# Hybrid SSD and attention block: decay sums placed behind z, one group's norm factors a weight run later, rotary channels swapped by two transfers

## The chip, the cores and the metric

The kernel runs on one core of one Trainium2 chip. The metric is the device time of one execution in microseconds (us), as the median of three runs. The profile is of one further execution.

## The reference

One layer over 256 tokens of width 1024, in float32. An RMS norm is followed by one wide input projection whose columns feed two branches and their gates: a Mamba-2 mixer (8 groups, 32 heads, two chunks of 128 tokens) and an attention with partial rotary embedding (16 heads of 64 channels). Both branches are projected, weighted with sigmoid gates, added, projected once more and added to the input; a gated conv FFN of width 2816 and a last norm follow. Cut to what the change touches:

```python
dt = softplus(dt_raw + dt_bias);  A = -exp(a_log)
A_cs = cumsum(dt * A)                      # inside each chunk of 128 tokens
L = exp(A_cs[l] - A_cs[s])  for s <= l     # decay factors of the scan
y = ssd_scan(X, dt, A, B, C) + X * d_skip
y = y * silu(z)
y = y * rsqrt(mean(y * y over the group's 256 channels) + eps) * norm_w

rot, rest = t[..., :16], t[..., 16:]       # q and k, per head of 64 channels
rot_half = concat([-rot[8:], rot[:8]])
t = concat([rot * cos + rot_half * sin, rest])
```

The attention uses q and k only in the product over a head's 64 channels, so any order of these channels serves if it is the same in q and k.

## The kernel before

Channels lie on the 128 partitions and tokens along the free axis. Weights stream from HBM in units of 1 MB (`raw`, eight tiles of 128 x 256 columns, three buffers, loaded by SP in the order of `seq`). Each unit is split in two halves: ScalarE copies the rounded part (`hi`, line 94) and VectorE subtracts it (`lo`, line 95); there are four buffers of each, that is two units. The split of a unit is traced two units ahead (`next_unit`). A product takes three matmuls for each tile, hi times hi, hi times lo and lo times hi (lines 151 to 153 with the weight as the stationary operand, 169 to 171 with the tokens stationary). So a unit of `mm_unit` is 48 matmuls with 256 columns.

TensorE's order is the order of the program (`manual_schedule`). On VectorE, ScalarE and GpSimd a planner chooses the order when the kernel is built; a block under `high_priority` goes ahead of other work that is ready, and `issue_after` puts instructions behind a named one. Each of these engines then works off its own list in that order.

For each of eight groups g TensorE runs `u_bc` (B and C), `u_x`, the small matmuls `small_1`, `u_qk`, then `u_z`, and in odd groups `u_v`, in even groups a quarter of the gates in four steps (`u_gate`: two units, each step one half unit), with `small_2` between them. `small_1(g)` works on the scan output of the group before (`s_y`), its scores (`a_s`), and, one group further back, on the attention output (`a_o`) and the norm factors (`s_pb`). `small_2(g)` has the score products and decay factors of the scan (`s_cb`), the transposed x (`s_xt`), the sums of squares of the group before (`s_st`) and its transposed probabilities (`a_t`).

Group 0 is special, since the decay sums are made there for all heads. `dt_chain` (line 483) computes `dtw` on VectorE from u_x(0) on, `dt_sums` (line 508) sums it over tokens with the matmuls of lines 510 and 511, `dt_turn` (line 516) transposes the sums, copies them to `acsT` (line 521) and sends them to HBM (line 522); `load_acs` (line 302) reads the rows of a group back to all partitions (`acsB`, one buffer, line 304). `s_cb` makes twelve decay steps per group from `acsB` on ScalarE (lines 365 and 367) and one over all (368). TensorE's order in group 0 is u_bc(0), the dt matmuls, u_x(0), u_qk(0), `dt_sums`, u_z(0), `dt_turn`, steps 1, 2, 3 of the gate, `small_2(0)`, step 4. The bias of the gates is loaded on GpSimd's queue right behind the swap transfers (line 585, two of 1 MB).

The norm factors of a group come in two steps. `s_st` sums squares and starts a chain of small VectorE steps that ends in `ry` (line 195). `s_pb` spreads `ry` over the partitions with two fp32 matmuls into `pb` (line 215, four instructions in the trace); VectorE multiplies (line 408) and the result is split into `yn` (lines 177 and 178). Behind the last group come `small_1(8)`, the first run of `w_ssd` (which uses `yn` 0 to 3), `small_2(8)`, the second run, `s_pb(7)`, `a_o(7)`, and the third and fourth; `yn` of group 6 is used in the fourth.

The rotation is done in `u_qk` and `turn_qk`. ScalarE copies q and k to `qkraw` (line 311), GpSimd issues DMAs that write the partner rows into `swap` (lines 314 and 315), and VectorE multiplies by cosine (318), and later by sine (325), and adds (326). Before, the 16 rotated channels of a head are its first 16 rows, partners 8 rows apart.

Of the kernel before, what the change touches and what calls it, by code (L numbers as in the profile page):

```python
# [18 lines left out]
P = 128  # L19
# [3 lines left out]
NG = 8  # L23
# [16 lines left out]
def block_kernel(tc, xtok_d, par_d, nf_d, con_d, rope_d, wdt_d, win_d, wgate_d, bg_d, watt_d, wssd_d, wout_d, wup_d, wdn_d, out_d):  # L40
    nc = tc.nc
    st = ExitStack()
    pool = lambda name, bufs=1, **kw: st.enter_context(tc.tile_pool(name=name, bufs=bufs, **kw))
    with st:
        const = pool("const")
        wpool = pool("w")
        pairs = pool("pairs")
# [8 lines left out]
        rope = const.tile([P, 2, T], F32, name="rope")  # L56
# [249 lines left out]
        def u_qk(g):  # L306
            hv = next_unit()
            ps = mm_tile()
            mm_unit(ps, hv, hn)
            raw = atp.tile([P, 2, T], F32, tag="qkraw", bufs=1, name="qkraw")  # L310
            S[g]["qk_copy"] = nc.scalar.activation(raw, ps, AF.Copy)
            sw = swaps[g % 2]
            for o in (0, 64):
                nc.gpsimd.dma_start(sw[o : o + 8], raw[o + 8 : o + 16])
                nc.gpsimd.dma_start(sw[o + 8 : o + 16], raw[o : o + 8])
            qk = S[g]["qk"] = atp.tile([P, 2, T], F32, tag="qk", bufs=2, name="qk")
            cosb = rope[:, 0:1, :].to_broadcast([P, 2, T])
            nc.vector.tensor_tensor(qk, raw, cosb, op=ALU.mult)

        def turn_qk(g):  # L320

            sw, qk = swaps[g % 2], S[g]["qk"]
            sinb = rope[:, 1:2, :].to_broadcast([P, 2, T])
            with tc.issue_after(split_unit.last.ins):
                nc.vector.tensor_tensor(sw, sw, sinb, op=ALU.mult)
                nc.vector.tensor_tensor(qk, qk, sw, op=ALU.add)
# [77 lines left out]
        def s_pb(g):  # L404
            rb = rms_bcast(S[g]["ry"])
            yg = S[g]["yg"]
            for m in range(2):
                nc.vector.scalar_tensor_tensor(yg[:, m], yg[:, m], col(C_NW + 2 * g + m), rb, op0=ALU.mult, op1=ALU.mult)
                p = new_pair("yn")
                split_pair(p, yg[:, m])  # L410
                yn[2 * g + m] = p
# [27 lines left out]
        def a_t(g):  # L439
            S[g]["pt"] = []  # L440
            for j in range(2):
                pt_ps = ps_s.tile([P, 4, P], F32, tag="at", bufs=2, name="pt_ps")
                for b in range(3):
                    nc.tensor.transpose(pt_ps[:, b], S[g]["pr"][j][:, b], ident)  # L444
                pt = atp.tile([P, 3, P], F32, tag="pt", bufs=2, name="pt")
                nc.scalar.activation(pt, pt_ps[:, 0:3], AF.Copy)
                S[g]["pt"].append(pt)
# [60 lines left out]
        def dt_sums():  # L508
            ps_a = ps_s.tile([P, 2, T], F32, tag="ss", bufs=2, name="ps_a")
            nc.tensor.matmul(ps_a[:, 0, 0 : 2 * NH], tri, dtw[:, 3], start=True, stop=True)  # L510
            nc.tensor.matmul(ps_a[:, 0, 2 * NH : 3 * NH], ones, dtw[:, 3, 0:NH], start=True, stop=True)
            with tc.high_priority():
                nc.vector.tensor_copy(flat(acs), ps_a[:, 0, 0 : 2 * NH])
                nc.vector.tensor_tensor(alm, ps_a[:, 0, 2 * NH : 3 * NH], acs[:, 0, :], op=ALU.subtract)
# [45 lines left out]
        def small_1(g):  # L560
            if 0 <= g - 1 < NG:
                s_y(g - 1)
                a_s(g - 1)
            if 0 <= g - 2:
                a_o(g - 2)
                s_pb(g - 2)

        def small_2(g):
            if g < NG:
                s_cb(g)  # L570
                s_xt(g)
            if 0 <= g - 1:
                s_st(g - 1)
                a_t(g - 1)

        for g in range(NG):
            if g:
                u_bc(g)
                u_x(g)
                small_1(g)  # L580
                load_acs(g)
            u_qk(g)
            if g == 0:
                for c in range(2):
                    tc.keep_in_program_order(nc.gpsimd.dma_start(gates[:, c], bg_d.partition_broadcast(P)))
                dt_sums()
                u_z(g)
                turn_qk(g)
                dt_turn()
                load_acs(0)  # L590
                gate = u_gate(0)
                next(gate)
                next(gate)
                next(gate)
                small_2(g)
                next(gate)
            elif g == NG - 1:
                u_z(g)
                turn_qk(g)
                small_2(g)  # L600
                u_v(g)
            elif g % 2:
                u_v(g)
                turn_qk(g)
                u_z(g)
                small_2(g)
            else:
                u_z(g)
                turn_qk(g)
                gate = u_gate(g // 2)  # L610
                next(gate)
                next(gate)
                small_2(g)
                next(gate)
                next(gate)
# [216 lines left out]
def _layout(i):  # L832

    f = {k: np.asarray(v) for k, v in i.items()}
    rows = lambda a: np.ascontiguousarray(a)
    vec = lambda a: a.reshape(-1, P).T
    cw = f["ssd_conv_w"][0]
    fw = f["ffn_conv_w"][0]
    par = np.concatenate(
        [  # L840
            vec(f["norm1_w"][0]), vec(f["norm2_w"][0]), np.zeros((P, 8), np.float32),
            vec(f["ssd_norm_w"][0]), vec(np.repeat(f["ssd_d"][0], 64)),
            cw.reshape(4, 32, P).transpose(2, 1, 0).reshape(P, 128), vec(f["ssd_conv_b"][0]),
            fw.reshape(3, NF, P).transpose(2, 1, 0).reshape(P, 3 * NF), vec(f["ffn_conv_b"][0]),
            np.broadcast_to(f["ssd_dt_bias"][0], (P, NH)), np.broadcast_to(f["ssd_a_log"][0], (P, NH)),
        ],
        axis=1,
    )
    w = f["w_in"][0]
    oz, ox, odt = 0, 2048, 6144  # L850
    oq = odt + NH
    ok, ov, og = oq + 1024, oq + 2048, oq + 3072
    a = np.arange(P)
    b = np.arange(256)
    units = np.zeros((5, NG, 256), np.int64)
    for g in range(NG):
        units[0, g] = np.r_[ox + 2048 + g * P + a, ox + 3072 + g * P + a]
        units[1, g] = ox + 256 * g + b
        units[2, g] = np.r_[oq + g * P + a, ok + g * P + a]
        units[3, g] = ov + 256 * (g % 4) + b  # L860
        units[4, g] = oz + 256 * g + b
    cols = units.reshape(-1, 256)

    def tiles(wm, cols):

        n = cols.shape[0]
        return rows(wm[:, cols.reshape(-1)].reshape(-1, P, n, 256).transpose(2, 1, 0, 3))

    def tiles512(wm):

        n = wm.shape[1] // 512
        return rows(wm.reshape(-1, P, n, 512).transpose(2, 1, 0, 3)).reshape(n, P, -1, 256)

    up = np.stack([np.r_[m * P + a, FH + m * P + a] for m in range(NF)])
    s, l = np.arange(P)[:, None], np.arange(P)[None, :]
    tri = (s <= l).astype(np.float32)
    neg = np.where(l <= s, np.float32(0), np.float32(-1e30)).astype(np.float32)
    con = np.stack([np.eye(P, dtype=np.float32), tri, np.ones((P, P), np.float32), tri, neg, np.zeros((P, P), np.float32), neg], axis=1)
    con = np.concatenate([con.reshape(P, 7 * P), np.tile(np.eye(NH, dtype=np.float32), (4, 1))], axis=1)
    inv = np.float32(500000.0) ** (-np.arange(0, 16, 2, dtype=np.float32) / np.float32(16))  # L880
    ang = np.arange(T, dtype=np.float32)[:, None] * inv[None, :]
    rope = np.zeros((P, 2, T), np.float32)
    rope[:, 0] = 1.0
    for o in (0, 64):
        rope[o : o + 8, 0] = rope[o + 8 : o + 16, 0] = np.cos(ang).T
        rope[o : o + 8, 1] = -np.sin(ang).T
        rope[o + 8 : o + 16, 1] = np.sin(ang).T
    return [
        ("xtok", f["x"][0].reshape(2, P, D).transpose(1, 0, 2)),
        ("par", par),  # L890
        ("nf", f["norm_f_w"]),
        ("con", con),
        ("rope", rope),
        ("wdt", w[:, odt : odt + NH].reshape(KD, P, NH).transpose(1, 0, 2)),
        ("win", tiles(w, cols).reshape(5, NG, P, KD, 256)),
        ("wgate", tiles512(w[:, og : og + 2 * D])),
        ("bg", f["b_gate"][0]),
        ("watt", tiles512(f["w_att_proj"][0])),
        ("wssd", tiles512(f["w_ssd_proj"][0])),
        ("wout", tiles512(f["w_out"][0])),  # L900
        ("wup", tiles(f["w_ffn_up"][0], up)),
        ("wdn", tiles512(f["w_ffn_down"][0])),
    ]
# [18 lines left out]
```

## Time and profile before

| | |
|---|---|
| median of 3 runs | 609.34 us (609.33 to 609.73) |
| the profiled execution | 610.12 us, of which the span is 608.3 |
| busy: TensorE / weight load | 592.5 us (97%) / 547.1 us (90%) |
| busy: VectorE / ScalarE / GpSimd | 463.2 us (76%) / 361.7 us (59%) / 26.5 us (4%) |
| mean granted TensorE clock | 0.99 |
| DMA | 109.79 MB, 180 GB/s over the span |

The span is the time from the first to the last instruction. Busy shares are means over stages with different limits, so the waits of the busiest engine, and what ended them, are read next, then the timelines of the engines around those waits. A timeline row gives the start, the duration, the engine, the line, what is written and read, and in brackets how long the engine had been idle and what ended it. TensorE's matmuls are pipelined, so the time between two starts tells more than a row's duration.

### The profile page before, as it was taken

Reading aid. Unit: us, or ns where it says so; the run is one execution under the profiler, and the core shown is the slowest. Engines: PE = TensorE matmul, PEld = TensorE weight load, DVE = VectorE, ACT = ScalarE, POOL = GpSimd, SP = SyncE. Lnnn points to the kernel's source line nnn. Section 1 sums busy time; section 2 is a strip of 40 time slices with the busy share of each in tenths; the row PEclk is TensorE's granted clock in tenths of the full one; section 3 lists DMA queues with packets and bytes.
Section 4 is the critical chain, followed back from the end, with each engine's and each line's share of the span. In section 5 each row is a group of like instructions: output and inputs, shape, how many; then the busy total and the mean of one; then the engine's idle time right before and its main releaser. Section 6 shows DMA issues by size and latency. Waiting matters only on the chain.

```text
span 608.3 us, 10705 instructions
## 1 busy us (share of the span) xinstructions
PE 592.5 (97%) x4206; PEld 547.1 (90%) x4206; DVE 463.2 (76%) x891; ACT 361.7 (59%) x654; POOL 26.5 (4%) x51
## 2 busy tenths in 40 slices
PE   8969999999999999999999999999999999999995
PEld 7968999989999999999998888889999999998884
DVE  5864979978799797987988546667988888885543
ACT  6625678765778667686686334456655555554532
POOL 0021010100101001010010000000000000000100
PEclk9979999999999999999999999999999999999998
DMA  8665645365453644635325755545455454464611
GB/s 329 231 259 193 217 160 183 101 225 198 145 179 134 226 159 143 218 138 204 139 85 199 260 197 200 188 162 201 149 201 183 168 204 170 143 217 165 219 58 70
DMA packets 18244, 109.79 MB, mean 180 GB/s; under 512 B 2689, under 2 KB 3073, under 8 KB 6161
## 3 DMA queue, kind: packets, MB, share of 16 engines
q1 hardware_dynamic: 15264, 100.42, 47.1%
q0 software_dynamic: 2496, 6.85, 3.2%
q10 hardware_dynamic: 432, 1.84, 0.7%
q8 instruction: 33, 0.54, 0.4%
q14 instruction: 19, 0.15, 0.1%
HBM read 107.49 MB, written 1.08 MB: 178 GB/s over the span
## 4 chain that ended last, share of the span: by engine, by line
PE 92%; DVE 3%; ACT 2%; DMA 1%; issue 1%; POOL 0%; DVEq 0%; ACTq 0%; POOLq 0%
PE mm L151 16%; PE mm L152 16%; PE mm L153 16%; PE mm L169 11%; PE mm L171 10%; PE mm L170 10%; PE py L392 2%; PE s_ps L421 1%; DVE lo L95 1%; PE mm L339 1%; PE mm L338 1%; PE mm L337 1%; PE po L458 1%; PE pb L215 1%; PE pt_ps L444 1%
## 5 line engine op out<-in xcount | busy, mean ns | idle before, releaser
L94 ACT ACTIVATE hi<-raw 128x1024 fp32r<-128x1024 f32 x186 | 195.7, 1058 | 181.9 <-PE mm L152 100.6
L95 DVE TENSOR_TENSOR lo<-raw,hi 128x1024 fp32r<-128x1024 f32 x186 | 226.9, 1225 | 89.9 <-ACT hi L94 89.2
L151 PE MATMUL mm<-hn,hi 128*128 128x256 f32 x512 | 147.1, 287 | 0.0
L152 PE MATMUL mm<-hn,hi 128*128 128x256 f32 x512 | 146.1, 285 | 0.4 <-DVE hn L225 0.4
L153 PE MATMUL mm<-hn,lo 128*128 128x256 f32 x512 | 145.8, 285 | 0.0
L151 PEld LDWEIGHTS mm<-hn,hi 128*128 128x128 f32 x512 | 99.3, 194 | 0.9 <-issue 0.4
L152 PEld LDWEIGHTS mm<-hn,hi 128*128 128x128 f32 x512 | 99.3, 194 | 0.9 <-DVE hn L225 0.8
L151 PE MATMUL mm<-xw,hi 128*128 128x256 f32 x352 | 99.8, 283 | 0.0
L152 PE MATMUL mm<-xw,hi 128*128 128x256 f32 x352 | 99.6, 283 | 0.0
L153 PE MATMUL mm<-xw,lo 128*128 128x256 f32 x352 | 99.6, 283 | 0.0
L153 PEld LDWEIGHTS mm<-hn,lo 128*128 128x128 f32 x512 | 99.3, 194 | 0.0
L152 PEld LDWEIGHTS mm<-xw,hi 128*128 128x128 f32 x352 | 67.6, 192 | 0.0
L151 PEld LDWEIGHTS mm<-xw,hi 128*128 128x128 f32 x352 | 67.6, 192 | 0.0
L153 PEld LDWEIGHTS mm<-xw,lo 128*128 128x128 f32 x352 | 67.6, 192 | 0.0
L277 DVE SCALAR_TENSOR_TENSOR cacc<-mm,par,cacc 128x255 f32<-128x255 f32 (+2 forms) x96 | 44.5, 477 | 2.2 <-ACT cacc L273 1.4
L170 PE MATMUL mm<-lo,act 128*128 128x512 f32 (+1 forms) x92 | 35.0, 380 | 0.0
L169 PE MATMUL mm<-hi,act 128*128 128x512 f32 (+1 forms) x92 | 34.9, 380 | 0.0
L171 PE MATMUL mm<-hi,act 128*128 128x512 f32 (+1 forms) x92 | 34.9, 380 | 0.0
L169 PE MATMUL mm<-hi,hn 128*128 128x512 f32 x64 | 25.4, 397 | 0.0
L169 PE MATMUL mm<-hi,yn 128*128 128x512 f32 x64 | 25.2, 394 | 0.0
L170 PE MATMUL mm<-lo,hn 128*128 128x512 f32 x64 | 25.0, 390 | 0.0
L171 PE MATMUL mm<-hi,hn 128*128 128x512 f32 x64 | 25.0, 390 | 0.0
(188 smaller groups left out, 966.2 us busy)
## 6 DMA issues: line engine op xcount, KB each, us to landing
raw<-in_win_dram SPq DMA_DIRECT2D x35, 1024.0 KB, 4.8
raw<-in_wup_dram SPq DMA_DIRECT2D x22, 1024.0 KB, 4.8
raw<-in_wdn_dram SPq DMA_DIRECT2D x10, 1024.0 KB, 4.8
raw<-in_wgate_dram SPq DMA_DIRECT2D x8, 1024.0 KB, 5.1
raw<-in_wssd_dram SPq DMA_DIRECT2D x8, 1024.0 KB, 4.8
acsB<-acsT_d POOLq DMA_DIRECT2D x8, 512.0 KB, 4.9
raw<-in_watt_dram SPq DMA_DIRECT2D x4, 1024.0 KB, 5.0
raw<-in_wout_dram SPq DMA_DIRECT2D x4, 1024.0 KB, 5.0
```

The lines of the kernel that those rows point to most:

```text
L94: nc.scalar.activation(hi[:, :n], raw[:, k0 : k0 + n], AF.Copy)
L95: split_unit.last = nc.vector.tensor_tensor(lo[:, :n], raw[:, k0 : k0 + n], hi[:, :n].bitcast(F32), op=ALU.subtract)
L151: nc.tensor.matmul(ps[m], wh, xh, start=a, stop=False)
L152: nc.tensor.matmul(ps[m], wh, xl, start=False, stop=False)
L153: nc.tensor.matmul(ps[m], wl, xh, start=False, stop=z)
L169: nc.tensor.matmul(o, xh, wh, start=(k == 0 if apart else k0 + k == 0), stop=False)
L170: nc.tensor.matmul(o, xh, wl, start=False, stop=False)
L171: nc.tensor.matmul(o, xl, wh, start=False, stop=(k0 + k == nk - 1))
L215: nc.tensor.matmul(pb[:, 0, c * P : c * P + P], y[:, c : c + 1].to_broadcast([P, P]), ident, start=True, stop=True)
L277: nc.vector.scalar_tensor_tensor(acc[:, s:], src[:, m, : T - s], w(m, 3 - s), acc[:, s:], op0=ALU.mult, op1=ALU.add)
L337: nc.tensor.matmul(ps[:, c, :], xh, hi[:, kk], start=(k == 0 and c == 0), stop=False)
L392: nc.tensor.matmul(o, xt[:, c, r, :], rhs, start=(c == 0), stop=(c == 1))
```

## The change

It has three parts.

1. In group 0, `dt_sums` comes behind `u_z` and `turn_qk`, and the first step of the gate is placed between `dt_sums` and `dt_turn` with its `load_acs`. TensorE's order becomes u_qk(0), u_z(0), `dt_sums`, gate step 1, `dt_turn`, steps 2 and 3, `small_2(0)`, step 4.
2. Behind the last group, `s_pb(6)` leaves `small_1(8)` and stands at the end of `small_2(8)`, that is behind the first run of `w_ssd`.
3. The rows of q and k are permuted in the weights: a head's 16 rotated channels lie on partitions 48 to 63 (first head of the tile) or 64 to 79 (second), with partners in neighbouring rows. Two DMAs per group, each of 16 rows with a step of two, take the place of four DMAs of 8 rows; the tables of sine and cosine follow.

```diff
-            for o in (0, 64):
-                nc.gpsimd.dma_start(sw[o : o + 8], raw[o + 8 : o + 16])
-                nc.gpsimd.dma_start(sw[o + 8 : o + 16], raw[o : o + 8])
+            nc.gpsimd.dma_start(sw[48:80:2], raw[49:80:2])
+            nc.gpsimd.dma_start(sw[49:80:2], raw[48:80:2])
...
                 a_o(g - 2)
-                s_pb(g - 2)
+                if g < NG:
+                    s_pb(g - 2)
...
             if 0 <= g - 1:
                 s_st(g - 1)
                 a_t(g - 1)
+            if g == NG:
+                s_pb(g - 2)
...
-                dt_sums()
                 u_z(g)
                 turn_qk(g)
+                dt_sums()
+                gate = u_gate(0)
+                next(gate)
                 dt_turn()
                 load_acs(0)
-                gate = u_gate(0)
-                next(gate)
                 next(gate)
                 next(gate)
                 small_2(g)
...
+    pairs = np.arange(16).reshape(2, 8).T.reshape(-1)
+    turn = np.r_[np.arange(16, 64), pairs, 64 + pairs, np.arange(80, P)]
...
-        units[2, g] = np.r_[oq + g * P + a, ok + g * P + a]
+        units[2, g] = np.r_[oq + g * P + turn, ok + g * P + turn]
...
-    for o in (0, 64):
-        rope[o : o + 8, 0] = rope[o + 8 : o + 16, 0] = np.cos(ang).T
-        rope[o : o + 8, 1] = -np.sin(ang).T
-        rope[o + 8 : o + 16, 1] = np.sin(ang).T
+    for o in (48, 64):
+        rope[o : o + 16 : 2, 0] = rope[o + 1 : o + 16 : 2, 0] = np.cos(ang).T
+        rope[o : o + 16 : 2, 1] = -np.sin(ang).T
+        rope[o + 1 : o + 16 : 2, 1] = np.sin(ang).T
```

## Rows read from the trace of the kernel before

**Rows 1.** The page: the span, and the busy time of the engines.

```profile
span 608.3 us, 10705 instructions
...
PE 592.5 (97%) x4206; PEld 547.1 (90%) x4206; DVE 463.2 (76%) x891; ACT 361.7 (59%) x654; POOL 26.5 (4%) x51
```

**Rows 2.** Waits of TensorE: total us, times, longest us.

```profile
PE ps_a L510 <- DVE dtw L506: 4.8, 1, 4.8
...
PE pb L215 <- DVE ry L195: 0.6, 1, 0.6
```

**Rows 3.** Timeline of TensorE, 32 to 50 us.

```profile
32.70 0.28 PE L153 MATMUL mm<-hn,lo 128*128 128x256 f32 x1
37.76 0.66 PE L510 MATMUL ps_a<-dtw,con 128*128 128x64 f32 x2 [4.77 <-DVE dtw L506]
...
38.60 0.56 PE L151 MATMUL mm<-hn,hi 128*128 128x256 f32 x1
...
46.72 0.38 PE L519 MATMUL ps_t<-con,acs 128*32 128x128 f32 x2
...
49.71 0.39 PE L169 MATMUL mm<-hi,hn 128*128 128x512 f32 x1
```

**Rows 4.** Stretches: busy of PE, PEld, DVE, ACT, POOL; PEclk, DMA share, GB/s.

```profile
37.00:38.00 1.00, 0.24 (x2) 0.28 (x2) 0.57 (x3) 0.00 (x0) 1.00 (x3) 0.50 0.17 31
...
43.00:44.00 1.00, 1.00 (x8) 1.00 (x7) 0.00 (x0) 0.11 (x1) 0.00 (x0) 0.59 1.05 442
```

**Rows 5.** Timeline of TensorE: starts of bc(1), of x(1), its first lo.

```profile
59.00 0.28 PE L151 MATMUL mm<-hn,hi 128*128 128x256 f32 x1
...
64.76 0.28 PE L151 MATMUL mm<-hn,hi 128*128 128x256 f32 x1
...
65.00 0.28 PE L153 MATMUL mm<-hn,lo 128*128 128x256 f32 x1
```

**Rows 6.** Timeline of VectorE, 24 to 68 us: lo splits and the end of `dt_chain`.

```profile
27.79 1.22 DVE L95 TENSOR_TENSOR lo<-raw,hi 128x1024 fp32r<-128x1024 f32 x1 [0.38 <-ACT hi L94]
...
37.38 0.22 DVE L506 TENSOR_TENSOR dtw<-dt,nega 128x64 f32<-128x64 f32 x1
...
47.90 1.23 DVE L95 TENSOR_TENSOR lo<-raw,hi 128x1024 fp32r<-128x1024 f32 x1 [1.68 <-ACT hi L94]
...
62.98 4.62 DVE L95 TENSOR_TENSOR lo<-raw,hi 128x1024 fp32r<-128x1024 f32 x4
```

**Rows 7.** Timeline of GpSimd, 30 to 70 us: DMA issues.

```profile
37.29 1.11 POOL L585 DMA_DIRECT2D gates<-in_bg_dram  x2
48.41 0.53 POOL L522 DMA_DIRECT2D acsT_d<-acsT  x1 [10.01 <-ACT acsT L521]
50.44 0.55 POOL L304 DMA_DIRECT2D acsB<-acsT_d  x1 [1.50 <-DMA acsT_d<-acsT]
```

**Rows 8.** Timeline of ScalarE, 24 to 66 us: first decay step, next split.

```profile
56.10 0.70 ACT L365 ACTIVATE mx<-acsB,acs 128x128 f32<-128x128 f32 x2 [2.36 <-DMA acsB<-acsT_d]
...
60.58 1.04 ACT L94 ACTIVATE hi<-raw 128x1024 fp32r<-128x1024 f32 x1
```

**Rows 9.** The tile `swap`: one of its two issuing lines (ns), and its transfers.

```profile
L314 POOL DMA_DIRECT2D swap<-qkraw x16: 512/518/694, 35.1 to 307.4; - x16
...
DMA to landing us min/median/max: 1.7/1.8/5.0
```

**Rows 10.** Line 585, the gate biases: from issue to landing.

```profile
DMA to landing us min/median/max: 7.2/8.2/9.1
```

**Rows 11.** Timeline of TensorE, 316 to 328 us.

```profile
318.37 0.87 PE L458 MATMUL po<-pt,vt 128*64 128x256 f32 x8
319.87 0.71 PE L215 MATMUL pb<-con,ry 128*128 128x128 f32 x4 [0.62 <-DVE ry L195]
...
326.25 0.85 PE L444 MATMUL pt_ps<-con,pr 128*128 128x128 f32 x6
```

**Rows 12.** Timeline of ScalarE, 318 to 331 us: the last probabilities of group 7.

```profile
325.32 0.79 ACT L436 ACTIVATE pr<-pr,sm 128x128 f32<-128x128 f32 x2
```

## The prediction

> **What bounds the kernel now.** I read the page's busy times first: TensorE is busy for 592.5 of 608.3 us [rows 1], so a change pays only where TensorE stands still or runs slowly; VectorE (76%) and ScalarE (59%) matter through what TensorE waits for. Second, the list of TensorE's waits. After the start-up it names two: 4.8 us for the decay products `dtw` ahead of `ps_a`, and 0.6 us for group 6's norm factor `ry` ahead of `pb` [rows 2]. No wait of TensorE names a swap. Third, TensorE's timeline around the long wait [rows 3]: the last matmul of qk(0) starts at 32.70, the next instruction at 37.76, z(0) at 38.60, and the transposes `ps_t` at 46.72. z(0) took 8.12 us, while the same 48 matmuls of bc(1) took 64.76 - 59.00 = 5.76 us [rows 5]. The reason is the granted clock: it is 0.50 in the stretch from 37 to 38 us, that is the 1.2 GHz level, after TensorE had been idle for 4 us, and full again only near 44 us [rows 4]. So this hole costs its idle time and a slow z. Fourth, the timelines of VectorE, GpSimd and ScalarE, to see who is late once TensorE is early [rows 6 to 8].
>
> **Part 1, the decay sums behind z.** What is moved is two matmuls of `dt_sums` (with the two VectorE steps that read them) past z's 48 matmuls, and two transposes of `dt_turn` past the first quarter-step of the gate, with the ScalarE copy and the two GpSimd DMAs that follow them (`acsT_d` out, `acsB` back). On SP nothing moves in program order.
>
> Can z start when qk ends? One matmul step is 0.12 us (5.76 / 48), so TensorE is free at 32.82. The lo half of z's second half-unit started at 27.79 and took 1.22 us, so all of z's operands exist by 29.0 [rows 6]. So z runs from 32.82 to 38.58, at full clock, because TensorE was never idle. `dtw` was done at 37.38 + 0.22 = 37.60 [rows 6], a microsecond ahead of z's end. Three terms are removed:
> - idle time, 37.76 - 32.82 = 4.94 us;
> - the slow clock in z, 8.12 - 5.76 = 2.36 us;
> - the slow clock in `ps_a`: it took 38.60 - 37.76 = 0.84, at twice the clock an estimated 0.42.
>
> That is 7.7 us; I take 7.6, since one more change between short and long matmuls is made (0.1, estimated).
>
> **What is late next.** TensorE's whole schedule moves up by 7.7, but the decay sums' round trip does not. `ps_t` plus the gate's first step take 49.71 - 46.72 = 2.99 us [rows 3]; the step alone is about 2.85. So `ps_t` now starts at 38.58 + 0.42 + 2.85 = 41.9 instead of 46.72: 4.85 earlier, which is 2.85 less than TensorE. On ScalarE the twelve decay steps of `s_cb(0)` are queued behind `acsB`; it waited 2.36 us for that and started at 56.10 [rows 8]. Behind them came the hi split of x(1), at 60.58, and VectorE's lo splits from 62.98, four in 4.62 us: the first was done at 64.14, the second at 65.30 [rows 6, 8]. TensorE wanted the first at 65.00 [rows 5] and the second 24 matmuls later, at 67.88: slack was 0.86 and 2.6. Afterwards it wants them at 57.3 and 60.2, while `acsB` is there at 56.10 - 4.85 = 51.25 at best. The cover of this chain is nearly used up, and what is left depends on two things.
>
> The first is the order on ScalarE, which the diff doesn't fix: the planner chooses it. The buffer for x(1)'s first hi comes free after the gate's third step, and the round trip now starts one step (2.85 us) closer to that point. So the split can come ahead of the decay steps (order B) or stay behind them (order A). Under A the first lo is ready 64.14 - 56.10 = 8.04 after `acsB`, at 59.3: a wait of 2.0. Under B the first is early and the second is ready at 51.25 + 9.2 - 1.16 = 59.3, 0.9 ahead of need. I take B: before, the buffer was free at about 49.71 + 2 x 2.85 = 55.4 and `acsB` there at 56.1, less than 1 us apart; now it is 47.7 against 51.25 or later.
>
> The second is how much later `acsB` lands, call it c. The write `acsT_d` was issued at 48.41, when GpSimd's queue was empty, and its read at 50.44 [rows 7]. Now the write is issued at 43.56. The two gate-bias loads, 1 MB each, were issued on the same queue from 37.29 and landed up to 9.1 us after issue [rows 7, 10], so until about 46.9; two swap issues fewer (0.52 each [rows 9]) bring that to 45.9, and SP's next weight load, which waits for a lo split that ended at 49.13 [rows 6] and now ends near 41, brings 1 MB beside them: 2.4 us at the 442 GB/s of that stretch [rows 4], so 48.3. Low end: the write is not held, c = 0 (the swaps' small transfers mostly land in 1.8 us [rows 9]). High end: the write lands with the last gate bias, and the read is issued at 48.6 instead of 45.6, c = 3.0; a swap that met other traffic did take 5.0 us [rows 9]. I take the middle, 1.5. Under B the wait is then 1.5 - 0.9 = 0.6 us; the ends are 0 and 2.1.
>
> The Trainium skill, page "DMA: Bandwidth & Descriptors", section "Queues, rings and completion order", speaks against the change here: within one queue of a DMA engine descriptors start in order, and the engine alternates between queues by whole packets. By that rule the write stands behind all that is left of the gate biases; no row of before shows a small transfer behind a large one on GpSimd's queue, so no trace here tells yet.
>
> **Part 2, group 6's norm factors.** The four `pb` matmuls leave the place behind `po(6)` and come after the transposes `pt_ps(7)`, one weight run later. The wait before them goes: 0.62 us [rows 11]. `ry` was ready just before 319.87, and the new place is some 6 us later. The work is moved, not removed: the matmuls cost the same there, and VectorE's and ScalarE's steps on `yn` move along; their user, the fourth run of `w_ssd`, is two runs off. What is late next: `pt_ps(7)` started at 326.25 and needs probabilities that ScalarE finished at 325.32 + 0.79 = 326.11 [rows 11, 12]. TensorE gets there about 1 us earlier, but so does ScalarE, roughly, since the `yn` steps no longer stand ahead of them. Ends 0.2 and 0.62; I take 0.5, near the upper one.
>
> **Part 3, two swap transfers.** Sixteen issues of GpSimd go away, 0.52 us each [rows 9], off TensorE's path: worth 0, between -0.1 and 0.1 us, because the rotated values are used a whole stage later. If the second transfer, which writes the rows between those of the first, were made to wait for it, it would cost about 1.8 us on GpSimd only, hidden by the same distance. The permuted weights and tables have the same sizes. Cover gone, it could hold up VectorE, which has a stage in hand.
>
> **The sum.** The profiled execution took 610.12 us (span 608.3 and 1.82 around it), 0.78 above the median of the runs. The terms come off either: 609.34 - 7.6 - 0.5 + 0.6 - 0 = 601.6, and 0.2 for small new gaps that TensorE's earlier arrival may open elsewhere (between 0 and 0.8): **601.8**.
>
> **The rivals.**
> - Order A stays. For: it is what the planner chose before [rows 8]. Against: the split is now ready sooner, relative to `acsB`. TensorE waits 2.0 + c = 3.5 at x(1): 609.34 - 8.1 + 3.5 = 604.7, between 603.2 and 606.2.
> - The write is held to the end: order B with c = 3.0, the high end above, a wait of 2.1 instead of 0.6 in x(1): 603.3. For: it shares its queue with 2 MB that are still on the way [rows 7, 10]. Against: transfers of this size mostly land in 1.8 us. By the rule of queue order of the Trainium skill, page "DMA: Bandwidth & Descriptors", this is the case.
> - `dtw` is late, so that part of the wait stays in front of `ps_a`. z's first half frees a split buffer at about 35.7, so ScalarE and VectorE begin the gate's second unit while the last steps of `dt_chain` run. One or two lo splits of 1.22 ahead of them put `dtw` at 38.8 or 40.0, against 38.58: 0.3 to 1.5 us, hence 602.1 to 603.3. Against: the chain has high priority, and had interleaved steps in before too.
> - Slower. Order A, and both the write and the read of the round trip meet loads, the read as the slowest swap did (5.0 instead of 1.8 [rows 9]): c = 1.5 + 3.2 = 4.7, a wait of 6.7. TensorE's clock had fallen after 4 us of idleness [rows 3, 4], so the slow stretch comes back at x(1), at 2.36 + 0.42 = 2.8. Together 9.5 against 8.1: 610.7. It decides from c = 3.3 on. Against: the queues would have to collide twice.
>
> **How the numbers follow.** The forecast (B, small waits, 600.8 to 602.6) has 0.39, the write held to the end 0.13, the late `dtw` 0.13, order A 0.25, slower 0.03; 0.04 lies below 600.8 (no new wait at all and all of 7.7 + 0.62), and 0.03 between 608.1 and 610.5. From 600.8 to 605.5 it holds 0.39 + 0.13 + 0.13 and two thirds of order A, 0.82. About 0.2% (1.2 us) is what a measurement of this kernel can tell from no change; all cases but the slower one and the last lie beyond it on the fast side: faster 0.94, same 0.03, slower 0.03.
>
> **What would show it.** Right: no wait for `dtw`, z(0) in 5.76 us, a granted clock of 1.0 from 37 to 44 us, `ps_t` near 42, step two of the gate near 42.0, no wait ahead of `pb`, and bc(1) at about 51.3. Order A or B is read from ScalarE's timeline: is the hi split ahead of or behind the decay steps; c is read from the wait of the first decay step. Wrong: a new TensorE wait for a `lo` in x(1) of more than 2 us, a clock of 0.5 around 60 us, a wait for `dtw` near 38.6, or a new wait in the `w_ssd` runs.

## The result and the profile after

The changed kernel takes 604.36 us (median of 5 runs, 603.99 to 606.36), the kernel before 609.73 beside it (609.33 to 610.08). The ratio is 0.9919, with a 95% interval from 0.9902 to 0.9936: 0.8% faster. The forecast was 601.8 with a range of 600.8 to 605.5, so the sign and the range held, and the point was 2.6 us too low.

| | before | after |
|---|---|---|
| profiled execution, us | 610.12 | 604.52 |
| its span, us | 608.3 | 602.7 |
| granted TensorE clock, mean | 0.990 | 0.996 |
| `bc(1)` starts, us | 59.00 | 51.43 |
| `py(0)`, the work behind x(1), starts | 70.61 | 65.19 |
| last normalise of ScalarE starts | 603.26 | 597.15 |

The page of after: the span, and the busy time of each engine, as in [rows 1].

```profile
span 602.7 us, 10673 instructions
...
PE 589.3 (98%) x4206; PEld 543.5 (90%) x4206; DVE 462.0 (77%) x891; ACT 362.2 (60%) x654; POOL 18.0 (3%) x35
```

TensorE's waits of after, as in [rows 2]. Both waits of [rows 2] are gone. Two new ones stand there, for the hi and the lo split of a weight.

```profile
PE mm L151 <- ACT hi L94: 0.9, 1, 0.9
PE mm L153 <- DVE lo L95: 0.8, 1, 0.8
```

TensorE's timeline of after, to be laid beside [rows 3, 5] (start us, duration us). The decay sums follow z without a wait at 38.65, the gate's first step starts at 39.09, the transposes `ps_t` at 41.90 instead of 46.72, and step two at 42.04 instead of 49.71. The row at 51.43 is the first of bc(1): 7.57 us earlier than before. Of that 0.12 is an earlier start of this execution, since the last matmul of qk(0), the first row, starts at 32.58 instead of 32.70. The rows at 61.10 and 62.36 lie in the middle of x(1), and each has its wait in brackets.

```profile
32.58 0.28 PE L153 MATMUL mm<-hn,lo 128*128 128x256 f32 x1
...
38.65 0.41 PE L509 MATMUL ps_a<-dtw,con 128*128 128x64 f32 x2
...
39.09 0.48 PE L169 MATMUL mm<-hi,hn 128*128 128x512 f32 x1
...
41.90 0.38 PE L518 MATMUL ps_t<-con,acs 128*32 128x128 f32 x2
42.04 0.48 PE L169 MATMUL mm<-hi,hn 128*128 128x512 f32 x1
...
51.43 0.28 PE L151 MATMUL mm<-hn,hi 128*128 128x256 f32 x1
...
61.10 0.39 PE L151 MATMUL mm<-hn,hi 128*128 128x256 f32 x1 [0.88 <-ACT hi L94]
...
62.36 0.39 PE L153 MATMUL mm<-hn,lo 128*128 128x256 f32 x1 [0.76 <-DVE lo L95]
...
65.19 1.09 PE L391 MATMUL py<-mx,xt 128*64 128x256 f32 x10
```

The stretch of [rows 4] in after (busy us of PE, PEld, DVE, ACT, POOL; granted clock, DMA share, GB/s). The clock is 1.00 where it was 0.50 to 0.59. The DMA engines are 95% busy.

```profile
37.00:44.00 7.00, 6.97 (x41) 5.89 (x40) 5.52 (x11) 2.87 (x4) 0.43 (x2) 1.00 0.95 367
```

ScalarE's timeline of after, for [rows 8]. The hi split of x(1)'s first half, at 47.77, stands ahead of the decay steps, the second half's behind them, from 60.00. In between ScalarE waits 5.58 us for `acsB`.

```profile
47.77 1.06 ACT L94 ACTIVATE hi<-raw 128x1024 fp32r<-128x1024 f32 x1 [1.60 <-PE mm L171]
54.42 0.74 ACT L364 ACTIVATE mx<-acsB,acs 128x128 f32<-128x128 f32 x2 [5.58 <-DMA acsB<-acsT_d]
...
60.00 2.94 ACT L94 ACTIVATE hi<-raw 128x1024 fp32r<-128x1024 f32 x3
```

GpSimd's timeline of after, for [rows 7], with the round trip of the decay sums. The wait of 5.03 us in the second row is the landing of the write.

```profile
43.76 0.52 POOL L521 DMA_DIRECT2D acsT_d<-acsT  x1 [6.57 <-ACT acsT L520]
49.32 0.55 POOL L304 DMA_DIRECT2D acsB<-acsT_d  x1 [5.03 <-DMA acsT_d<-acsT]
```

TensorE's timeline of after around group 6's norm factors, for [rows 11]. `pb` stands behind `pt_ps`, and no row has a wait.

```profile
312.95 0.87 PE L457 MATMUL po<-pt,vt 128*64 128x256 f32 x8
319.68 0.85 PE L443 MATMUL pt_ps<-con,pr 128*128 128x128 f32 x6
320.37 0.61 PE L215 MATMUL pb<-con,ry 128*128 128x128 f32 x4
```

The tile `swap` of after, for [rows 9]: on this line 8 issues instead of 16, and the landings.

```profile
L314 POOL DMA_DIRECT2D swap<-qkraw x8: 487/487/492, 35.6 to 301.2; - x8
...
DMA to landing us min/median/max: 1.6/1.7/3.7
```

So the account of the two profiled executions is this. bc(1) comes 7.57 us earlier. py(0) comes 5.42 earlier (70.61 - 65.19), so 2.15 are lost in x(1): 0.88 and 0.76 of waits, and the rest at their edges. The last normalise comes 6.11 earlier, so 0.69 are gained at `pb`. The span is 5.6 shorter, so 0.5 is lost in the last output transfers. (From the start of the last normalise to the end of the span the profiled executions of this text's kernels took 5.08 to 5.94 us, so this 0.5 is not shown to come from the change.) 7.57 - 2.15 + 0.69 - 0.51 = 5.60 = 610.12 - 604.52.

### The profile page after: what moved, and what is told of

Its sections match the earlier page's. It is cut to its first block, busy times and chain, and to the rows that moved or that the text cites. A ratio compares the mean times of both kernels' runs of the same rounds, so it can differ in the third digit from the quotient of the medians.

```text
span 602.7 us, 10673 instructions
## 1 busy us (share of the span) xinstructions
PE 589.3 (98%) x4206; PEld 543.5 (90%) x4206; DVE 462.0 (77%) x891; ACT 362.2 (60%) x654; POOL 18.0 (3%) x35
## 4 chain that ended last, share of the span: by engine, by line
PE 94%; DMA 2%; ACT 1%; DVE 1%; issue 1%; ACTq 0%; DVEq 0%
PE mm L151 17%; PE mm L153 17%; PE mm L152 17%; PE mm L169 10%; PE mm L170 10%; PE mm L171 10%; PE py L391 2%; PE mm L336 1%; PE mm L337 1%; PE mm L338 1%; PE s_ps L420 1%; PE po L457 1%; PE pt_ps L443 1%; DMA acsT_d<-acsT 1%; PE pb L215 1%; DMA acsB<-acsT_d 1%
## 5 line engine op out<-in xcount | busy, mean ns | idle before, releaser
L151 PEld LDWEIGHTS mm<-hn,hi 128*128 128x128 f32 x512 | 98.2, 192 | 2.0 <-ACT hi L94 1.4
L152 PEld LDWEIGHTS mm<-hn,hi 128*128 128x128 f32 x512 | 98.2, 192 | 0.9 <-DVE hn L225 0.8
L169 PE MATMUL mm<-hi,hn 128*128 128x512 f32 x64 | 25.5, 398 | 0.0
L364 ACT ACTIVATE mx<-acsB,acs 128x128 f32<-128x128 f32 x64 | 22.1, 394 | 5.6 <-DMA acsB<-acsT_d 5.6
```

What stands on the lines that cost most here:

```text
L151: nc.tensor.matmul(ps[m], wh, xh, start=a, stop=False)
L152: nc.tensor.matmul(ps[m], wh, xl, start=False, stop=False)
L169: nc.tensor.matmul(o, xh, wh, start=(k == 0 if apart else k0 + k == 0), stop=False)
L364: nc.scalar.activation(mx[:, r, b], acsB[:, r, c * P : c * P + P], AF.Relu, scale=-1.0, bias=acs[:, c, h : h + 1])
```

## The experiments

**Each part alone.** Three kernels take the parts one by one. The first is part 1.

```
-                dt_sums()
                 u_z(g)
                 turn_qk(g)
+                dt_sums()
+                gate = u_gate(0)
+                next(gate)
                 dt_turn()
                 load_acs(0)
-                gate = u_gate(0)
-                next(gate)
                 next(gate)
```

> Part 1 alone, with the four swap transfers and the old place of the norm factors. If the gain of the whole change is the closed hole minus a new wait at x(1), this kernel has bc(1) start 7.6 us earlier than before, a wait of 2 to 3.2 us in the second half of x(1) (the gate biases are issued 1 us later than in the changed kernel, so the write of the decay sums can only land later), and 0.6 us of waiting left ahead of pb: 4.4 to 5.5 us faster than before. If parts 2 or 3 carry a share of their own, the gain here is under 4 us.

Measured: 606.73 us (606.37 to 606.82) against 610.19 for before beside it, a ratio of 0.9935 (0.9912 to 0.9959). That is 3.5 us faster, under the 4.4 to 5.5 expected. TensorE's waits in its trace:

```profile
PE mm L151 <- ACT hi L94: 1.1, 1, 1.1
PE mm L153 <- DVE lo L95: 0.8, 1, 0.8
...
PE pb L215 <- DVE ry L195: 0.7, 1, 0.7
```

The waits in x(1) belong to part 1. The wait of `pb` is still there. Its trace also starts later: TensorE's clock was 0.57 from 8 to 12 us where after has 1.00, and its first weight matmul comes at 13.59 instead of 11.95. So its span, 604.9 us, is 2.2 longer than after's: 1.64 from the late start, 0.24 more in x(1) and 0.77 behind py(7), where `pb` waits, less 0.47 in the last output transfers. Without the late start the gain would be 5.1 (an estimate: 3.46 + 1.64), inside what was expected. Why its start-up met the lower clock is open.

The second kernel is part 2.

```
                 a_o(g - 2)
-                s_pb(g - 2)
+                if g < NG:
+                    s_pb(g - 2)
...
+            if g == NG:
+                s_pb(g - 2)
```

> Part 2 alone. If the wait of 0.62 us ahead of pb is simply gone (the changed kernel's trace gives 0.69 between py(7) and pb(7)): 0.6 to 0.7 us faster than before and no new wait of TensorE. Rival: the wait comes back at the transposes of the probabilities or in the third run of w_ssd, then under 0.2 us.

Measured: 609.47 us (608.61 to 610.37), ratio 0.9987 (0.9975 to 0.9999). `pb` does not wait, and the distance from py(7) to pb(7) is 15.71 us instead of 16.35 in before, so 0.64 is gained. There is no new wait in the `w_ssd` runs.

The third is part 3, with the permuted weights and tables that belong to it.

```
-            for o in (0, 64):
-                nc.gpsimd.dma_start(sw[o : o + 8], raw[o + 8 : o + 16])
-                nc.gpsimd.dma_start(sw[o + 8 : o + 16], raw[o : o + 8])
+            nc.gpsimd.dma_start(sw[48:80:2], raw[49:80:2])
+            nc.gpsimd.dma_start(sw[49:80:2], raw[48:80:2])
```

> Part 3 alone. If the rotation is off TensorE's path: within 0.3 us of before, the wait of 4.8 us for dtw still there, 16 swap issues fewer on GpSimd. Rival: GpSimd's earlier queue pulls the gate biases and with them the decay sums forward; that would show as an acsB earlier than before, but TensorE doesn't wait for it there, so no time either.

Measured: 609.75 us (608.97 to 610.29), ratio 0.9992 (0.998 to 1.0004). The median can't be told from no change. The trace shows something else: the wait of `pb` is gone here too, although `pb` stands where it stood. VectorE's timeline of before and then of this run, around the last swap:

```profile
312.04 0.69 DVE L325 TENSOR_TENSOR swap<-swap,rope 128x512 f32<-128x512 f32 x1 [0.77 <-DMA swap<-qkraw]
...
319.66 0.16 DVE L195 SCALAR_TENSOR_TENSOR ry<-ra,ry 128x2 f32<-128x2 f32 x1
```

```profile
310.43 0.69 DVE L324 TENSOR_TENSOR swap<-swap,rope 128x512 f32<-128x512 f32 x1
...
318.66 0.15 DVE L195 SCALAR_TENSOR_TENSOR ry<-ra,ry 128x2 f32<-128x2 f32 x1
```

In before VectorE stood still for 0.77 us for the swap, with the steps that make `ry` queued behind. The last of the four swap transfers of before was issued 0.15 us ahead of a weight load of SyncE and took 4.0 us to land, where most take 1.8:

```profile
307.89 0.52 POOL L315 DMA_DIRECT2D swap<-qkraw  x1
```

```profile
308.04 0.33 SPq L84 DMA_DIRECT2D raw<-in_wssd_dram  x1
```

With two issues instead of four the last goes out at 306.49, well ahead of that load, and lands in 1.7 us, `ry` is done 1.00 us earlier, and `pb` starts at 319.08 right behind `po`. The distance from py(7) to pb(7) is 15.64 us: the same 0.7 as with part 2.

**Parts 1 and 3 without part 2.** The edit is the second diff above, undone in the changed kernel.

> Parts 1 and 3 of the change without part 2: group 6's norm factors are spread where they were before. In the run of part 3 alone VectorE did not wait for the swap at 312 and the factor ry came 0.99 us earlier, so that the broadcast pb met it. Theory (parts 2 and 3 each remove the same wait of 0.62 to 0.69 us, so that part 2 adds nothing on top of part 3): no PE wait for ry, pb(7) about 15.6 us behind py(7), the time of the whole change within 0.3 us. Rival (part 2 has a gain of its own): a PE wait for ry of 0.5 to 0.7 us, the time 0.5 to 0.7 us above the whole change.

Measured: 604.44 us (604.21 to 607.17); the whole change gave 605.71 (604.37 to 607.36) beside it. The medians are 1.3 us apart, not the 0.3 expected, since the whole change scatters (below); the shortest executions, 604.21 and 604.37, are 0.16 apart. The distance from py(7) to pb(7) is 15.65 us, as in after (15.66). `pb` follows `po` without a wait:

```profile
312.72 0.87 PE L457 MATMUL po<-pt,vt 128*64 128x256 f32 x8
313.52 0.71 PE L215 MATMUL pb<-con,ry 128*128 128x128 f32 x4
```

Parts 2 and 3 each remove the same wait. On top of part 3, part 2 adds nothing that can be measured.

**What holds the write of `acsT`?** The prediction thought of the gate biases ahead of it in GpSimd's queue (theory Q). In after the last of them landed 9.2 us after its issue at 36.66, at 45.8, and the write at 49.0, 3.2 us later. That doesn't fit. The rival, theory E: the write lands with the 1 MB weight load that SyncE had issued 1.7 us before it. First the biases are taken out of the way.

```
         gates = const.tile([P, 2, 2 * D], F32, name="gates")
+        for c in range(2):
+            tc.keep_in_program_order(nc.gpsimd.dma_start(gates[:, c], bg_d.partition_broadcast(P)))
...
             if g == 0:
-                for c in range(2):
-                    tc.keep_in_program_order(nc.gpsimd.dma_start(gates[:, c], bg_d.partition_broadcast(P)))
```

> The changed kernel with the two gate-bias loads issued some 8 us earlier, right after the swap buffers are cleared. Theory Q (the write of the decay sums stood behind the gate biases in GpSimd's queue): the write lands 1.7 to 2.5 us after its issue instead of 5.3, acsB is there near 51.2 instead of 54.4, ScalarE's order being the same the second half of x(1) is split in time, TensorE's wait of 2.1 us at x(1) is gone: 2.1 us faster than the changed kernel, near 602.2. Theory E (the write is slow because the 16 DMA engines are full, and SP's weight load that follows the lo split at 42 us is enough for that): the write still takes 4 us or more, and the gain over the changed kernel is under 0.8 us.

Measured: 603.80 us (603.53 to 604.22), ratio 0.9889 (0.9869 to 0.9909). The biases were issued from 28.05 on, and the second had landed by 39.3. The write still took 5.2 us, and GpSimd's row for the read says so:

```profile
28.05 1.27 POOL L540 DMA_DIRECT2D gates<-in_bg_dram  x2
...
43.78 0.51 POOL L521 DMA_DIRECT2D acsT_d<-acsT  x1 [7.89 <-ACT acsT L520]
49.21 0.56 POOL L304 DMA_DIRECT2D acsB<-acsT_d  x1 [4.93 <-DMA acsT_d<-acsT]
```

Theory Q falls: nothing was left in GpSimd's queue ahead of the write. (The two swap transfers, which now stand behind the biases, took 4.5 and 4.2 us here instead of 1.8 and 1.7, and landed 0.2 and 0.3 us behind the second bias.) The next kernel changes the queue instead.

```
-                nc.gpsimd.dma_start(acsT_d, acsT)
+                nc.scalar.dma_start(acsT_d, acsT)
```

> The changed kernel with one edit: the 32 KB write of acsT is issued from ScalarE's queue, right behind the copy that fills it, instead of GpSimd's queue, in which the two gate-bias reads stand in front of it. Everything else is in the same order on every engine. In the changed kernel the write landed 5.3 us after its issue, the read acsB about 5 us later, ScalarE waited 5.58 us for it, and 604.36 us was the time. Theory E (the write shares the DMA engines with the 1 MB weight load that SyncE issued 1.8 us ahead of it, and lands only with that load, whichever queue it is in): landing 4.5 to 5.5 us after issue, ScalarE's wait 5.0 to 5.8 us, about 604.4 us. Theory Q (it is held behind the bias reads in GpSimd's own queue): landing 1.7 to 2.2 us after issue, the decay steps start near 51.3 instead of 54.42, no wait for x(1)'s split at 61 and 62, about 602.3 us.

Measured: 605.61 us (604.47 to 608.5), ratio 0.993 (0.9912 to 0.9949). From its DMA view (KB, us from issue to landing):

```profile
acsT_d<-acsT ACTq DMA_DIRECT2D x1, 32.0 KB, 5.4
```

Another queue, the same landing. (The read behind it took 6.8 us in this execution, its longest, so ScalarE waited 7.5 us instead of the 5.0 to 5.8 expected; more on that below.) Now the load is taken out of the way: the write goes into SyncE's queue, and the weight load of the unit behind x(1) is held behind it. TensorE, VectorE and ScalarE keep their order.

```
-                nc.gpsimd.dma_start(acsT_d, acsT)
+                dt_turn.write = nc.sync.dma_start(acsT_d, acsT)
...
-                raws.append(load_raw(*seq[len(raws)], step=KD if raws else 4))
+                with tc.issue_after(dt_turn.write.ins) if len(raws) == 8 else ExitStack(): raws.append(load_raw(*seq[len(raws)], step=KD if raws else 4))
```

> The changed kernel with the write of acsT put into SyncE's queue and the weight load of the unit behind x(1), which SyncE issued at 42.0, held behind it; PE, VectorE and ScalarE keep their order. The gate biases still move until 45.85 or a little before. Theory E (a write lands with the load issued just ahead of it): no load of weights is ahead but the one of 37.2, the write issued near 43.8 lands by 46 to 46.5 (2.0 to 2.7 us), the decay steps start near 51.3 to 52, ScalarE's wait falls from 5.58 to 2.5 to 3.2, at most 0.6 us of PE wait for x(1) is left, 602.2 to 602.9 us. Rival (the write is slow of itself in this stretch, by the other traffic or by its place): landing 5 us, about 604.4 us.

Measured: 602.62 us (602.48 to 604.06), ratio 0.9886 (0.9862 to 0.9909). The write lands in 2.7 us. ScalarE's first decay step, and the DMA view:

```profile
51.88 0.76 ACT L364 ACTIVATE mx<-acsB,acs 128x128 f32<-128x128 f32 x2 [2.94 <-DMA acsB<-acsT_d]
```

```profile
acsT_d<-acsT SPq DMA_DIRECT2D x1, 32.0 KB, 2.7
```

No wait of TensorE for x(1) is left, and py(0) starts at 63.13 instead of 65.19. The last kernel of this group is the same edit with the biases read early, so that nothing at all is in flight.

> The kernel with the gate biases read early (its write was issued at 43.78 and landed 5.2 us later, with a weight load issued at 43.1; 603.8 us), and in it the write put into SyncE's queue with that weight load held behind it. Nothing is then in flight when the write is issued. Theory E: the write lands 1.6 to 2.0 us after issue, near 45.6; acsB, which now shares the engines with the held load, lands near 50.8 to 52; ScalarE's wait for it is 2 to 3.3 instead of 5.28; PE's waits for x(1) fall from 1.4 to 0.6 or less; about 602.0 us. Rival (the write is slow for a reason that neither the biases nor the load gives): landing 5 us again, 603.8 us.

Measured: 602.86 us (602.76 to 604.41), ratio 0.989 (0.9866 to 0.9914). The write took 1.5 us:

```profile
acsT_d<-acsT SPq DMA_DIRECT2D x1, 32.0 KB, 1.5
```

Set side by side, with the youngest weight load that was in flight when the write was issued:

| kernel | write on | load in flight: issued, landed | write: issued, landed |
|---|---|---|---|
| before | GpSimd | none | 48.41, 50.2 |
| after | GpSimd | 42.02, 49.4 | 43.76, 49.0 |
| biases early | GpSimd | 43.05, 48.6 | 43.78, 48.9 |
| write on ScalarE's queue | ScalarE | 42.09, 48.7 | 43.60, 49.0 |
| load held behind | SyncE | 37.24, 46.1 | 43.60, 46.3 |
| load held behind, biases early | SyncE | none | 43.55, 45.0 |

In each case with a load in flight the write landed within 0.4 us of that load. Without one it took 1.5 to 1.7 us. In the four other kernels or executions here that issue the write behind that load (part 1 alone, parts 1 and 3, and the two that follow) it landed 0.2 to 0.4 us ahead of the load. Theory E stands. SyncE's queue without the held load was not tried; ScalarE's queue alone changed nothing. The Trainium skill, page "DMA: Bandwidth & Descriptors", section "Queues, rings and completion order", says that the write which reports a transfer as done lands only after every earlier write of the same DMA engine, across its queues; the landings on three queues agree with that. But not only the report was late, the 32 KB themselves were. With the write on ScalarE's queue, q10, its packets can be told from all others. The rows give packets, MB and the share of the engines' time for each queue, first from 42 to 47 us, then from 46.5 to 49. The write was issued at 43.60, and q10 has no row in the first stretch:

```profile
q1 hardware_dynamic: 206, 1.56, 75.4%
q0 software_dynamic: 78, 0.51, 24.2%
```

```profile
q1 hardware_dynamic: 83, 0.55, 66.0%
q10 hardware_dynamic: 48, 0.03, 4.0%
```

Its first packet moves at 47.05, 3.4 us after the issue, when most of the load's packets on q1 have moved; without a load in flight the first packet of the write moves 0.8 to 1.1 us after the issue. Why the engines served the load first is open.

**Can ScalarE's order help instead?** Both halves of x(1)'s split are put ahead of the decay steps of group 0, and group 0's small matmuls behind the gate's last step.

```
-                nc.scalar.activation(hi[:, :n], raw[:, k0 : k0 + n], AF.Copy)
+                split_unit.hi = nc.scalar.activation(hi[:, :n], raw[:, k0 : k0 + n], AF.Copy)
...
                 next(gate)
                 next(gate)
-                small_2(g)
                 next(gate)
+                load_to(8); units.append(split_unit(raws[7], seq[7][1])); small_2(g)
...
-            with tc.issue_after(S[g]["qk_copy" if g == NG - 1 else "z_tanh"].ins):
+            with tc.issue_after(S[g]["qk_copy" if g == NG - 1 else "z_tanh"].ins if g else split_unit.hi.ins):
```

> The changed kernel with ScalarE's order mended: both halves of x(1)'s weight split are put ahead of the decay steps of group 0, which wait for acsB; the small matmuls of group 0 move behind the last gate step. acsB should still come as late as in the changed kernel (decay steps near 54.4). Theory (the 2.15 us between bc(1) and py(0) that the changed kernel lost are the wait of x(1) for a split that stands behind the decay steps): the waits at 61 and 62 (0.88 and 0.76) are gone, py(0) is near 63.0 instead of 65.19, about 602.2 us. Rival (the decay steps themselves are late next: py(0) needs their mx, which VectorE writes behind them): PE waits for mx or the score product before py(0), the time stays within 0.5 us of 604.4.

Measured: 604.89 us (604.01 to 606.21), ratio 0.9913 (0.9886 to 0.9939). The median is the rival's, but TensorE does not wait where the rival has it. The waits in x(1) are gone, and py(0) starts at 64.62 in a trace that begins 1.62 us later than after's (the clock was 0.57 from 8 to 12 us, as in part 1 alone), so at 63.0 as expected. But the split of the next unit, qk(1), now stands behind the late decay steps, and TensorE waits there. The first decay step of ScalarE, and TensorE's wait:

```profile
57.97 0.69 ACT L364 ACTIVATE mx<-acsB,acs 128x128 f32<-128x128 f32 x2 [3.69 <-DMA acsB<-acsT_d]
```

```profile
PE mm L337 <- DVE lo L95: 2.0, 1, 2.0
```

This was the longest of the four executions, and its read `acsB` took 7.3 us where after's took 5.0. The decay steps start 1.9 us later than in after, once the late start is taken off, and that would by itself make nearly all of the wait of 2.0. So the waits of x(1) do come from splits behind late decay steps. That the new order only moves the wait to qk(1) is not shown: the late start and this wait make 3.6 of the 606.21 us, and no trace shows the order with a read of 5.0.

**The whole change and the held load, side by side.** Both kernels are taken as they are above, on one chip.

> The whole change, unedited, on the same chip and in the same rounds as its neighbours, so that they can be set against it: 604.4 us, ScalarE's wait for acsB near 5.6 us, PE's two waits for x(1) together near 1.6 us.

> The kernel with the write of acsT in SyncE's queue and the next weight load held behind it, unedited, beside the whole change on the same chip. Theory (the write's landing behind the load is all that keeps the change above 602.5 us): 1.5 to 2.2 us below the whole change, no PE wait for x(1). Rival (the difference between the two earlier calls was the chip's): within 0.5 us of the whole change.

Measured: the whole change 605.71 us (604.37 to 607.36, 6 runs), 1.3 above the 604.4 expected; the held load 602.64 (602.60 to 602.74, 4 runs). Against before the ratios are 0.9925 (0.9904 to 0.9947) and 0.9875 (0.9853 to 0.9897). The held load is 3.1 us faster, more than the 1.5 to 2.2 expected, because the whole change scatters; between the shortest executions it is 1.8. The held load is not free of scatter either: the four executions further up lie between 602.48 and 604.06. The profiled execution of the whole change was here its longest, 607.36: the read `acsB` took 6.5 us where it took 5.0 in the first trace, the decay steps started at 55.80, and TensorE waited longer. The first decay step of ScalarE, TensorE's timeline, and then two stretches:

```profile
55.80 0.76 ACT L364 ACTIVATE mx<-acsB,acs 128x128 f32<-128x128 f32 x2 [6.77 <-DMA acsB<-acsT_d]
```

```profile
62.48 0.39 PE L151 MATMUL mm<-hn,hi 128*128 128x256 f32 x1 [2.06 <-ACT hi L94]
...
63.74 0.39 PE L153 MATMUL mm<-hn,lo 128*128 128x256 f32 x1 [0.76 <-DVE lo L95]
...
66.06 0.41 PE L152 MATMUL mm<-hn,hi 128*128 128x256 f32 x1
```

```profile
60.00:61.00 1.00, 0.42 (x4) 0.21 (x2) 0.52 (x1) 1.00 (x3) 0.31 (x1) 1.00 0.00 0
...
65.00:66.00 1.00, 1.00 (x6) 1.00 (x6) 1.00 (x2) 1.00 (x2) 0.00 (x0) 0.50 0.65 213
```

The clock falls to 0.50, the 1.2 GHz level, after the stretch from 60 to 64 us, in which TensorE was busy for 1.2 us; a matmul takes 0.41 there instead of 0.28. py(0) starts at 67.89 instead of 65.19, 2.70 later, and the execution is 2.84 us longer. So this execution has the place and the mechanism of the prediction's slowest rival, a late read and a slow clock behind the holes, but under order B. No trace shows its other executions beside the held load. Why the read took 5.0 us in one execution and 6.5 in another is open: in the longer one the weight load issued 1.6 us ahead of it was slow too, 6.8 against 5.4.

## Why the prediction was right, and where it was off

**The gross gain: right.** 4.94 of idle time, 2.36 of slow z and 0.42 of slow `ps_a`, taken as 7.6 in all, were measured as 7.57 at bc(1), of which 0.12 is an earlier start. The clock was full throughout, as said. `ps_t` (41.90) and step two (42.04) came where they were put.

**`dtw`: right, by little.** A lo split of 1.22 us did slip in ahead of the last step of the chain, as the rival feared: that step ran at 38.28 instead of 37.38 and was done at 38.50, 0.15 us before `ps_a` started. One more split ahead of it and that rival would have been the case.

**Order B: right.** The split of x(1)'s first half went ahead of the decay steps, at 47.77. The formula of order B, a wait of c - 0.9, held as well: with the measured c it gives 2.3, and 2.15 were lost.

**The lateness c: the step that failed.** The prediction took 1.5, the middle of 0 and 3.0. Measured it is 54.42 - 51.25 = 3.2, above the upper end. So "The write is held to the end" came nearest, a rival with a chance of 0.13 and 603.3 us. That its size was nearly right is luck, since its reason was wrong: the prediction saw the weight load that would start near 41, but charged it as 2.4 us of delay to the gate biases in GpSimd's queue. With the biases gone the write was as late, on ScalarE's queue too, and with the load behind it the write was early. Its low end rested on the swaps' 1.8 us [rows 9] and on the write of before [rows 7]; it did not ask what these had in flight ahead of them, and the write of before had no load. Yet the trace of before held such a case: the 5.0 us of [rows 9], which the prediction put down to "other traffic", is a transfer of group 1 that was issued 0.14 us behind a weight load, and that group's four took 4.0 to 5.0 us. The load's issue, the first of the four, and the landings of the four:

```profile
81.67 0.33 SPq L84 DMA_DIRECT2D raw<-in_win_dram  x1
```

```profile
81.81 0.52 POOL L314 DMA_DIRECT2D swap<-qkraw  x1 [21.27 <-issue]
```

```profile
DMA to landing us min/median/max: 4.0/4.5/5.0
```

The rule of the Trainium skill that was weighed there (page "DMA: Bandwidth & Descriptors", section "Queues, rings and completion order"), order within one queue, does not account for the lateness, which was the same on another queue. The one about reports of completion, in the same section, agrees with the landings but does not say why the 32 KB themselves moved late.

**Part 2: size a little off, and shared.** 0.69 was measured in the whole change and 0.64 alone, 0.5 predicted. The sum took it once, and it is there once. But part 3 gives the same 0.7 without it.

**Part 3: the step "worth 0" was wrong taken alone.** The reason given, that the rotated values are used a whole stage later, holds for TensorE's use of them. It overlooked VectorE's own wait of 0.77 us at 312.04, with `ry` queued behind it and `pb` behind that. In the sum the miss costs nothing, since part 2 had taken that wait already.

**The rest.** No small gap opened on TensorE between 66 us and the last stretch (0.2 was taken), and 0.5 us were lost in the last output transfers, of which the prediction had nothing and which scatter by more than that. Against the forecast saving of 7.3 the measured 5.6 is 1.7 short: 1.55 from c (2.15 - 0.6), 0.51 at the end, less 0.19 of part 2 and 0.2 of gaps not met. The point was 2.6 us low in all. These make 1.7 of it. Another 0.24 is a slip in the sum: its terms give 609.34 - 7.6 - 0.5 + 0.6 = 601.84, not the 601.6 that was written. And 0.62 is the base: the terms were read in an execution of 610.12, 0.78 above the median that they came off, while after's profiled execution stood 0.16 above its own.

## What to carry to other kernels

When a change moves a small round trip through memory earlier, look at what every queue has in flight at its new time, not at its own queue alone: here a 32 KB write took 1.5 to 1.7 us in the clear and 5.0 to 5.7 behind a fresh 1 MB load in another queue, and issuing the load just behind the write, in one queue with it, was worth 3.1 us between the medians and 1.8 between the shortest executions. In two queues a short lead is not enough: a swap transfer 0.15 us ahead of a load took 4.0 us. The trace at hand may show the price already, as the swaps behind a load did here. When two edits aim at one wait, follow the wait's chain on the engine that ends it; both may remove the same 0.7 us. A reordering that takes a wait off one unit has to be followed to the next unit, whose split then stands behind what is late.

## What the runs showed of the hardware that was not expected

- A small write landed within 0.4 us of the large load that was in flight when it was issued, whether it was in GpSimd's, ScalarE's or SyncE's queue. Its data moved late, not only its report: on ScalarE's queue the first packet moved 3.4 us after the issue.
- Two holes of 2.06 and 0.76 us in x(1) brought TensorE's clock to 0.50 for some 3 us behind them (64.8 to 68.2 us). Holes of 0.88 and 0.76 at the same place, in after, left it at 1.00.
- The same kernel's `acsB` read, 512 KB, took 5.0 us in one execution and 6.5 in another; the second, with the slow clock behind its longer holes, was 2.8 us longer. With the load held behind the write the read took 5.2 and 5.5 us in two executions, and 6.8 where the biases were read early as well.
